# All transfers issued on one queue, and the last wait placed behind the closing barriers

The kernel runs on one core of a Trainium2 chip. The metric is the device time of one execution in microseconds, median of several runs; before the change 72.71 us.

Some words first. SP, ACT (ScalarE), VectorE, TensorE and GpSimd are the five engines; each works through its own list of instructions. SP, and here ACT too, issue transfers; 16 DMA engines then move the bytes in packets (those of the data are of 24,576 to 40,960 B in the kernel before). A transfer has landed when its semaphore, a counter that engines wait on, has been raised for all of it. At a barrier every engine waits for the others.

## The reference

A max-unpooling: every input element goes to one of the four places of a 2 x 2 block of the output, which `indices` names; the other three are zero.

```python
batch, channels, h, w = 16, 64, 32, 32            # kernel_size = 2
# x: float32 of that shape, indices: integers 0..3 (64 bit when they reach the kernel)
output = np.zeros((batch, channels, 2 * h, 2 * w), dtype=np.float32)
for b, c, i, j in ...:                            # cut: four nested loops
    idx = indices[b, c, i, j]
    output[b, c, 2 * i + idx // 2, 2 * j + idx % 2] = x[b, c, i, j]
```

In bytes: x 4.19 MB, indices 8.39 MB (the kernel reads all 64 bits and uses the low half), output 16.78 MB; 29.36 MB in all.

## The kernel before

The 1024 images lie on 128 partitions, eight per partition. SP loads x and then the last five images of indices; ACT loads the first three images of indices beside it. VectorE makes the output in 20 instructions, each the product of x and "index equals p" for one of the four places p. The output has four groups of two images; each is stored by SP with one transfer as soon as it is made. At the end SP waits for the stores, then two barriers over all engines close the program; those are added around the kernel and do not stand in its text.

```python
    with Program(nc) as program:
        program.first(nc.sync.dma_start(out=x_t, in_=x_v).then_inc(x_in, 16))
        program.first(nc.sync.dma_start(out=idx_t[:, cut:], in_=idx_v[:, cut:]).then_inc(idx_in[1], 16))
        program.first(nc.scalar.dma_start(out=idx_t[:, :cut], in_=idx_v[:, :cut]).then_inc(idx_in[0], 16))

        nc.vector.wait_ge(x_in, 16).then_inc(x_in, -16)
        for t in range(T):
            ...                    # cut: wait for idx_in at t = 0 and 3, for stored_0 at the last group
            for pidx in range(4):
                op = nc.vector.scalar_tensor_tensor(
                    out=o_c[:, k : k + n, :, pidx // 2, :, pidx % 2],
                    in0=idx_c[:, t : t + n], scalar=pidx, in1=x_c[:, t : t + n],
                    op0=mybir.AluOpType.is_equal, op1=mybir.AluOpType.mult)
            if k + n == G:
                op.then_inc(made, 1)

        for g in range(NG):
            nc.sync.wait_ge(made, g + 1)
            nc.sync.dma_start(out=out_v[g], in_=out_t[g]).then_inc(stored if g else stored_0, 16)
        nc.sync.sem_inc(made, -NG)
        nc.sync.wait_ge(stored, 16 * (NG - 1)).then_inc(stored, -16 * (NG - 1))
```

`program.first` puts a transfer ahead of the opening barrier, so that it starts at once: in the trace the issue of x starts at 0.00 us, the barrier's last semaphores at 1.2.

## Time and profile before

| | before |
|---|---|
| time, median (lowest to highest of 3) | 72.71 us (72.57 to 72.78) |
| the profiled execution: time / span | 72.79 / 71.00 us |
| part of the time outside the span | 1.79 us |
| VectorE busy | 35.6 us, half of the span |
| one packet of 32,768 B on one DMA engine | 1.213 us, 27.0 GB/s; 432 GB/s on 16 |

The span runs from the first recorded instruction to the end of the last one. The profile's lines on which the reading rests are in the prediction below; each "L" number is a line of the kernel that was profiled, so the same instruction has another number in another kernel.

### The profile page before, as it was taken

How to read it: one execution, taken by the hardware profiler on the slowest of the kernel's cores; microseconds unless marked ns; L12 is line 12 of the kernel's file. 1: busy time of each engine (PE TensorE's matmuls, PEld its weight loads, DVE VectorE, ACT ScalarE, POOL GpSimd, SP SyncE). 2: the span in 40 equal slices, each digit the busy share in tenths (PEclk: the TensorE clock that was granted, in tenths of full speed). 3: DMA queues.
4: the chain of work that ended last, by engine and by line, in shares of the span. 5: the costliest groups of instructions: out<-in, count | busy, mean ns of one | idle time of the engine just before them, and what ended most of it. 6: DMA issues, size and time to landing. Idle time of an engine off the chain costs nothing.

```text
span 71.0 us, 72 instructions
## 1 busy us (share of the span) xinstructions
DVE 35.6 (50%) x20; POOL 0.2 (0%) x4
## 2 busy tenths in 40 slices
DVE  0000000000089999999999999999999200000000
POOL 1000000000000000000000000000000000000000
DMA  9598997998988999879696989899898979696980
GB/s 277 240 434 378 517 498 314 443 462 378 563 369 369 462 577 438 369 314 572 295 591 295 517 369 517 369 425 462 369 517 351 535 314 572 295 591 295 517 369 0
DMA packets 1009, 29.36 MB, mean 414 GB/s; under 512 B 113, under 2 KB 113, under 8 KB 113
## 3 DMA queue, kind: packets, MB, share of 16 engines
q1 hardware_dynamic: 864, 26.21, 86.4%
q10 hardware_dynamic: 144, 3.15, 10.3%
q14 instruction: 1, 0.00, 0.0%
HBM read 12.58 MB, written 16.78 MB: 414 GB/s over the span
## 4 chain that ended last, share of the span: by engine, by line
DVE 45%; DVEq 4%; issue 1%
DVE out_t L127 45%; DVEq L175 4%
## 5 line engine op out<-in xcount | busy, mean ns | idle before, releaser
L127 DVE SCALAR_TENSOR_TENSOR out_t<-idx_t,x_t 128x2048 f32<-128x2048 int32 (+1 forms) x20 | 35.6, 1860 | 19.9 <-DVEq L116 19.9
L161 POOL MEMSET const-bfloat16-1.0<- 128x1 bf16 x1 | 0.1, 103 | 0.0
L161 POOL MEMSET const-uint8-127<- 128x1 uint8 x1 | 0.1, 102 | 0.0
L161 POOL MEMSET const-float32-1.0<- 128x1 f32 x1 | 0.1, 100 | 0.0
L161 POOL MEMSET const-float32-0.0<- 128x1 f32 x1 | 0.1, 99 | 0.2 <-issue 0.2
## 6 DMA issues: line engine op xcount, KB each, us to landing
out_dram<-out_t SPq DMA_DIRECT2D x4, 4096.0 KB, 13.5
idx_t<-in_indices_dram SPq DMA_DIRECT2D x1, 5120.0 KB, 31.2
x_t<-in_x_dram SPq DMA_DIRECT2D x1, 4096.0 KB, 19.5
idx_t<-in_indices_dram ACTq DMA_DIRECT2D x1, 3072.0 KB, 19.6
```

The lines of the kernel that those rows point to most:

```text
L127: op = nc.vector.scalar_tensor_tensor(out=o_c[:, k : k + n, :, pidx // 2, :, pidx % 2], in0=idx_c[:, t : t + n], scalar=pidx, in1=x_c[:, t ...
L161: nc = _bacc.Bacc("TRN2", target_bir_lowering=False, num_devices=1)
L175: with _tile.TileContext(nc) as tc:
```

## The change

Its intent is to let one engine issue all transfers in the order in which they are needed (x, three images of indices, five images, stores), and to let SP go through the closing barriers while the last stores still run, with the wait for them as SP's last instruction. The diff, with context cut:

```diff
+    def last(self, made):
+        def move(nc):
+            ins = self.block.instructions
+            at = next(k for k, i in enumerate(ins) if i.name == made.ins.name)
+            nc.main_func.blocks[-1].instructions.append(ins.pop(at))
+
+        self.nc.at_finalize(move)
...
         program.first(nc.sync.dma_start(out=x_t, in_=x_v).then_inc(x_in, 16))
-        program.first(
-            nc.sync.dma_start(out=idx_t[:, cut:], in_=idx_v[:, cut:]).then_inc(
-                idx_in[1], 16
+        for half, part in enumerate((slice(0, cut), slice(cut, None))):
+            program.first(
+                nc.sync.dma_start(out=idx_t[:, part], in_=idx_v[:, part]).then_inc(
+                    idx_in[half], 16
+                )
             )
-        )
-        program.first(
-            nc.scalar.dma_start(out=idx_t[:, :cut], in_=idx_v[:, :cut]).then_inc(
-                idx_in[0], 16
-            )
-        )
...
-        nc.sync.wait_ge(stored, 16 * (NG - 1)).then_inc(stored, -16 * (NG - 1))
+        program.last(
+            nc.sync.wait_ge(stored, 16 * (NG - 1)).then_inc(stored, -16 * (NG - 1))
+        )
```

## The prediction

> **What bounds the kernel now.** I read the page first (share of each engine, slices, queues), then the table of windows, the chain of waits, SP's own waits, and last the line and tile views of the closing instructions. The page:
>
> ```profile
> span 71.0 us, 72 instructions
> DVE 35.6 (50%) x20; POOL 0.2 (0%) x4
> ...
> DMA  9598997998988999879696989899898979696980
> ...
> HBM read 12.58 MB, written 16.78 MB: 414 GB/s over the span
> ```
>
> VectorE, the only computing engine, works half of the span; the DMA row is full from the third slice to the last but one. So this is a transfer kernel. The table of windows shows how even the transfers are (columns: stretch, length, VectorE and GpSimd busy, TensorE clock, DMA share, GB/s):
>
> ```profile
> 0.00:1.00 1.00, 0.00 (x0) 0.20 (x4) 1.00 0.00 0
> 1.00:2.90 1.90, 0.00 (x0) 0.00 (x0) 1.00 1.01 289
> 2.90:19.50 16.60, 0.00 (x0) 0.00 (x0) 1.00 1.04 449
> 19.50:31.20 11.70, 11.33 (x7) 0.00 (x0) 1.00 1.00 431
> 31.20:55.50 24.30, 24.27 (x14) 0.00 (x0) 1.00 1.01 434
> 55.50:69.50 14.00, 0.00 (x0) 0.00 (x0) 1.00 0.95 412
> 69.50:70.30 0.80, 0.00 (x0) 0.00 (x0) 1.00 0.01 0
> 70.30:71.00 0.70, 0.00 (x0) 0.00 (x0) 1.00 0.00 0
> ```
>
> A packet is booked whole in one stretch, so a stretch may be a few per cent off; the packet records say it better: every packet of 32,768 B takes 1.213 us and every one of 24,576 B takes 0.912 us, with no gap between packets of an engine, that is 27.0 GB/s on each of 16 engines, or 432 GB/s. All 29.36 MB at that rate need 67.95 us. The rest of the 71.0 us is the edges: 1.0 us until the first packet, a first packet that takes up to 2.33 us in place of 1.21, an offset of half a us between the engines, and the end. The reader is to see that only the two edges can be shortened; the 68 us between them hold the same bytes whatever their order.
>
> The page's chain of waits is of little use here:
>
> ```profile
> 41.63 2.83 DVEq L175
> 44.46 11.01 DVE out_t L127 x5
> ```
>
> It stops at VectorE's last result, at 55.5 us, and doesn't see the transfer behind it. SP's own waits and the two views of the end show the real one:
>
> ```profile
> SPq L144 <- SPq L144: 14.5, 1, 14.5
> SPq L175 <- PEq L175: 0.4, 2, 0.3
> ...
> L140 SPq DMA_DIRECT2D out_dram<-out_t x4: 333/338/347, 28.8 to 55.5; - x4
> ...
> DMA to landing us min/median/max: 12.6/13.5/14.8
> ...
> L144 SPq EVENT_SEMAPHORE  x1: 17/17/17, 70.3 to 70.3; - x1
> ...
> L175 POOLq EVENT_SEMAPHORE  x4: 17/17/17, 70.5 to 70.9; - x4
> ```
>
> The last store is issued at 55.5 us, lands 14.8 us later, at 70.3 us, and SP's wait for it passes at 70.3. Then come two closing barriers at 70.4 to 71.0 in which nothing moves. In the trace's records SP's wait ends at 70.343 and the last instruction of all, a barrier semaphore on TensorE's sequencer, at 71.002: 0.66 us.
>
> [...] from 2.9 to 19.1 us every DMA engine alternates a packet of x with one of the first indices, and the rate is the same 27 GB/s per engine that it has afterwards with SP's queue alone. [...] the last completion packet stands at 69.96 us and SP passes at 70.33, so 0.37 us of receipt stay with any order. [...] the profiled run took 72.79 us against a span of 71.0, so 1.79 us of the metric lie outside of it, and no run so far tells what they are.
>
> **The change part by part.**
>
> (a) The loads. Before, SP issues x (4.19 MB) and five images of indices (5.24 MB), ACT beside it three images of indices (3.15 MB). After, SP issues x, three images, five images. ACT loses one issue of 0.365 us; SP gets one more of about 0.4 us, ending near 1.3 us in place of 0.86. SP then arrives at the opening barrier at about 1.45 us, not 0.91. VectorE needs that barrier only at 19.6 us, so this costs nothing. VectorE's first instruction waits for both x and the first indices. Per engine these are 8 packets of 32 KiB and 8 of 24 KiB: 8 x (1.213 + 0.912) = 17.0 us of packets, interleaved or one behind the other. They end at about 19.1 to 19.4 us in both kernels; x now lands alone near 12.5 us in place of 19.5, but nobody uses it then. Worth to VectorE: 0, give or take 0.2.
>
> The five images end at 31.2 us in both. The first store is issued at 28.8 us, still ahead of the end of the loads; the four stores take 9.7 us each (8 packets per engine x 1.213 us), and are issued every 8.8 us, at 28.8, 37.9, 46.7 and 55.5. The last is issued 14.8 us ahead of its landing for 9.7 us of work: it waits some 4 us behind the third. So VectorE could even start 3 us later without an effect on the end. Order and queue are off the path. Sum of (a) in the steady part: 0.
>
> At the starting edge something might move. [...] the first packets of x take 1.67 to 2.33 us and not 1.21. If that is descriptors made in turn for two queues, the change gives back a part of about 0.5 us; if it is a first read that is slow anyway, nothing. I book -0.1 us.
>
> (b) SP's last wait. Before: wait at 70.33, then an SP drain, barrier one, barrier two, end at 71.00. After: SP passes both barriers right after the last issue, at about 56 to 57 us, beside the last store, which still has 13 us to run; then waits, and that is its last instruction. Removed from the path: 71.00 - 70.34 = 0.66 us on TensorE's queue, or 0.61 us if SP's own end counts (its last semaphore ended at 70.956). Added: 0; the wait itself (17 ns) was already there. The number of instructions and branches is the same.
>
> Sum: 72.71 - 0.66 - 0.1 = 71.95 us; the span from 71.00 to about 70.25. Against 72.71 that is -1.0%.
>
> **The rivals.**
>
> Rival 1: the tail is not in the metric as I read it. If the clock stops where the runtime has gathered all engines, then what four engines do after their last instruction could also move beside the last store, and the gain would exceed 0.66 us. For it: 1.79 us lie outside the span. Against it: SP is still last[...]. At most some 0.5 us more: 71.4. The opposite, that the barrier was already hidden, has nothing for it, because 0.66 us stand bare in the span; it would give 72.6.
>
> Rival 2: the start moves by more than I book. A clean first packet of 1.21 us on all engines, with descriptors not shared, could gain 0.5 us to 0.6 us: 71.45. For it: the first packets start at 1.00 to 2.00 us but end all at 2.90 to 3.40, as if held by one thing. Against it: that thing may be the first HBM access, which the change leaves.
>
> Rival 3: one queue is worse than two, for instance a gap where one transfer ends and the next begins[...]. Against it: in the trace the step from x to the five images on SP's queue shows 9 ns for the completion packet and no gap, and three stores stand in that queue behind each other at full rate. [...] With a gap of 0.3 us: 72.25.
>
> Rival 4: VectorE becomes the bound because its input lands later. It would need to start about 3 us later than 19.9; the byte count doesn't give that. 1 in 50; 73 or more.
>
> **Range and chances.** Rivals 1 and 2 pull down by up to 0.5 us each, rival 3 up by 0.3, and the median of three runs is good to 0.1 us (72.57 to 72.78). Hence 71.95 with 71.45 to 72.35 at 8 in 10. Faster by over 2% means under 71.26, a gain of 1.45 us: it needs 0.8 us beyond the tail, both rivals 1 and 2 together: 0.06. Slower by over 2% needs a stall the trace gives no hint of: 0.01. Within 2%: 0.93.
>
> **What would show it right or wrong.** Right: a span near 70.3; SP's last wait passing at 70.2 to 70.4 and being the last instruction; the barrier semaphores near 56 us; x landing at about 12.5 us and the first indices at about 19.5; VectorE starting at 19.6 to 20.0 and its 35.6 us unbroken; the same four landing times; packets of 1.213 us. Step (b) is wrong if the span falls by 0.66 us and the time doesn't, or the time falls by much more than the span. The starting edge is wrong if the first packets end clearly ahead of 2.9 us. The argument as a whole is wrong if the packets' rate differs with one queue or gaps appear between transfers.

## The result

| | before | after |
|---|---|---|
| time, median (lowest to highest of 4) | 72.69 us (72.57 to 72.78) | 71.60 us (71.46 to 71.86) |
| ratio, 95% interval | | 0.9855 (0.9824 to 0.9887) |
| the profiled execution: time / span | 72.79 / 71.00 us | 71.56 / 70.24 us |
| part outside the span | 1.79 us | 1.32 us |
| SP's last wait ends at | 70.343 us | 70.238 us |
| GpSimd's last instruction ends at | 70.914 us | 56.210 us |
| TensorE's last instruction ends at | 71.002 us | 56.298 us |

A ratio here is the mean time of one kernel's fast runs over that of the other's of the same rounds, so not quite the ratio of the medians quoted. The change gains 1.5%, about 1.1 us. The class is "within 2%".

The page of the changed kernel: VectorE's work is the same 35.6 us, the bytes are the same, and the span is shorter by 0.76 us.

```profile
span 70.2 us, 72 instructions
DVE 35.6 (51%) x20; POOL 0.2 (0%) x4
...
HBM read 12.58 MB, written 16.78 MB: 418 GB/s over the span
```

The windows of the changed kernel, in the stretches of the prediction (columns as there; the last but one is the DMA share, the last GB/s). From 1.0 to 69.5 us the rates differ by no more than a few packets that fall on one or the other side of a border; the 0.7 us without transfers at the end are gone.

```profile
1.00:2.90 1.90, 0.00 (x0) 0.00 (x0) 1.00 0.91 276
2.90:19.50 16.60, 0.00 (x0) 0.00 (x0) 1.00 1.04 450
19.50:31.20 11.70, 11.64 (x7) 0.00 (x0) 1.00 1.01 437
31.20:55.50 24.30, 23.96 (x14) 0.00 (x0) 1.00 1.00 432
55.50:69.50 14.00, 0.00 (x0) 0.00 (x0) 1.00 0.95 412
69.50:70.20 0.70, 0.00 (x0) 0.00 (x0) 1.00 0.01 0
```

The page's list of transfers (KB each, us from issue to landing), x and the three images of the kernel before first, then the changed kernel's loads. Before, x took 19.5 us and the three images 19.6 us, since their packets alternated (1.213 us for one of x, 0.912 for one of the images). Now x lands at 12.1 us, and nobody needs it then: VectorE also needs the three images, which land at 0.4 + 19.0 = 19.4 us. It starts at 19.56 us, before at 19.87.

```profile
x_t<-in_x_dram SPq DMA_DIRECT2D x1, 4096.0 KB, 19.5
idx_t<-in_indices_dram ACTq DMA_DIRECT2D x1, 3072.0 KB, 19.6
```

```profile
idx_t<-in_indices_dram SPq DMA_DIRECT2D x1, 5120.0 KB, 30.6
x_t<-in_x_dram SPq DMA_DIRECT2D x1, 4096.0 KB, 12.1
idx_t<-in_indices_dram SPq DMA_DIRECT2D x1, 3072.0 KB, 19.0
```

SP's own waits in the changed kernel (us in total, times, longest; L151 is the moved wait, L183 the closing barriers):

```profile
SPq L151 <- SPq L151: 14.0, 1, 14.0
SPq L183 <- PEq L183: 0.4, 2, 0.3
```

The line views of the moved wait and of the barriers in the changed kernel (count, duration in ns, first and last start in us). The wait still takes 14.0 us, but the barriers' GpSimd semaphores now stand at 55.8 to 56.2 us and not at 70.5 to 70.9, and L151 is the last thing of all.

```profile
L151 SPq EVENT_SEMAPHORE  x1: 17/17/17, 70.2 to 70.2; - x1
```

```profile
L183 POOLq EVENT_SEMAPHORE  x4: 17/17/17, 55.8 to 56.2; - x4
```

So the two traces show where the shorter span comes from. They do not show why the time fell by 1.1 us when the barriers' part in the span is only 0.66: the part outside the span fell too, from 1.79 to 1.32 us. That is the question of the experiments.

### The profile page after: what moved, and what is told of

Same layout as the page of the kernel before. It is cut to its first block, busy times and chain, and to the rows that moved or that the text cites. A ratio compares the mean times of both kernels' runs of the same rounds, so it can differ in the third digit from the quotient of the medians.

```text
span 70.2 us, 72 instructions
## 1 busy us (share of the span) xinstructions
DVE 35.6 (51%) x20; POOL 0.2 (0%) x4
## 4 chain that ended last, share of the span: by engine, by line
DVE 46%; DVEq 4%; issue 1%
DVE out_t L133 46%; DVEq L183 4%
## 5 line engine op out<-in xcount | busy, mean ns | idle before, releaser
L133 DVE SCALAR_TENSOR_TENSOR out_t<-idx_t,x_t 128x2048 f32<-128x2048 int32 (+1 forms) x20 | 35.6, 1857 | 19.6 <-DVEq L122 19.6
## 6 DMA issues: line engine op xcount, KB each, us to landing
x_t<-in_x_dram SPq DMA_DIRECT2D x1, 4096.0 KB, 12.1
```

The source lines that it names most:

```text
L133: op = nc.vector.scalar_tensor_tensor(out=o_c[:, k : k + n, :, pidx // 2, :, pidx % 2], in0=idx_c[:, t : t + n], scalar=pidx, in1=x_c[:, t ...
```

## The experiments

Twelve runs, in four calls on up to three chips (8, 6, 8 and 3); each ratio is against the kernel before in the same call. All outputs are right. "Outside" is the time less the span, as a mean over the runs with a span; the spans of the single runs are known to 0.1 us.

### Which part of the change gains

**The changed kernel again**, no edit, as the yardstick.

> The changed kernel once more, as the yardstick on this chip for the other runs of the call. All theories: some 1.05 us under the kernel before (ratio 0.9855 on record), a span near 70.2 to 70.5, and 1.3 to 1.4 us of the time outside the span (1.79 in the profiled run of the kernel before).

Measured: 71.60 us against 72.73, ratio 0.9841 (0.9825 to 0.9857), outside 1.32 us against a mean of 1.79 over the eleven runs of the kernel before (1.75 to 1.83). The gain and the smaller outside part are both steady.

**Only the wait moved**, loads as before:

```diff
-        nc.sync.wait_ge(stored, 16 * (NG - 1)).then_inc(stored, -16 * (NG - 1))
+        program.last(
+            nc.sync.wait_ge(stored, 16 * (NG - 1)).then_inc(stored, -16 * (NG - 1))
+        )
```

> Only the last wait moved behind the closing barriers; loads as before (ACT issues three images). Theory T (the tail makes all of it): ratio 0.985 to 0.987, span down by 0.66 us, time outside the span down from 1.79 to about 1.34. Theory A (ACT's missing transfer makes what lies outside the span shorter): only the span's 0.66 us, ratio 0.991, outside still 1.79. If the start gains 0.1 us by the loads, this run is 0.1 us slower than the changed kernel.

Measured: 71.69 us, ratio 0.9851 (0.9834 to 0.9868), outside 1.32 us. The moved wait alone makes 1.08 us of the changed kernel's 1.15 (means), and all of the smaller outside part. By the medians this run is 0.09 us slower than the changed kernel, which is what the expectation said of a start that gains 0.1 us; but the two intervals overlap, so the runs don't tell 0.1 us from nothing.

**Only the loads changed**, the wait ahead of the barriers as before:

```diff
-        program.last(
-            nc.sync.wait_ge(stored, 16 * (NG - 1)).then_inc(stored, -16 * (NG - 1))
-        )
+        nc.sync.wait_ge(stored, 16 * (NG - 1)).then_inc(stored, -16 * (NG - 1))
```

(against the changed kernel)

> Only the order of the loads and their issuer; SP waits for the stores ahead of the closing barriers as before. Theory T: ratio 0.998 to 1.001, outside the span 1.79 us. Theory A: ratio 0.993, outside the span about 1.34. Theory of the start (no second queue at the start, first packets quicker): 0.1 us or more off the span, ratio 0.998 or less.

Measured: 72.71 us, ratio 0.9996 (0.9982 to 1.001), outside 1.81 us. One queue in place of two, another order of landing, and ACT without a transfer are worth nothing that these runs can see: the interval is a gain of 0.13 us to a loss of 0.07, so a tenth of a microsecond is not excluded. The closing lines of this kernel look like those of the kernel before, with SP's wait (L150) at 70.2 and the barriers (L181) behind it, each from the view of its line:

```profile
L150 SPq EVENT_SEMAPHORE  x1: 17/17/17, 70.2 to 70.2; - x1
```

```profile
L181 POOLq EVENT_SEMAPHORE  x4: 17/17/17, 70.3 to 70.7; - x4
```

### Why the part outside the span shrinks

**All engines held to the end.** Added to the changed kernel (cut: the line that makes the semaphore `done`):

```diff
+        program.last(nc.sync.sem_inc(done, 4))
+        for engine in (nc.tensor, nc.vector, nc.scalar, nc.gpsimd):
+            program.last(engine.wait_ge(done, 1).then_inc(done, -1))
```

> The changed kernel, with the other four engines held to the end: after its wait SP adds 4 to a semaphore, and each of the four waits for it as its last instruction, about 0.05 to 0.1 us after SP. Theory E (0.45 us outside the span fell because four engines were done and out of the way 14 us earlier): outside the span back to about 1.79, time 72.1 to 72.2, ratio 0.993. Theory P (the part outside depends only on when SP is done): time only 0.05 to 0.1 us above the changed kernel, ratio 0.986 to 0.987, outside the span 1.3.

Measured: 72.28 us, ratio 0.9938 (0.992 to 0.9956), outside 1.82 us. Here no barrier follows SP's wait; its signal reaches the others within 0.14 us, and yet 0.7 us of the gain are gone. The lines of its end show that the four waits end together, right behind SP (L156 is the added wait; the profiled execution was the slowest of the six, hence 70.7 and not 70.4):

```profile
L156 POOLq EVENT_SEMAPHORE  x1: 17/17/17, 70.7 to 70.7; - x1
...
L156 PEldq EVENT_SEMAPHORE  x1: 51/51/51, 70.7 to 70.7; - x1
```

So it matters to the time outside the span when the other engines have their last instruction. The next four runs ask which of them. In each, one other engine makes the last wait alone, and SP is done at 56 us like the rest:

```diff
         program.last(
-            nc.sync.wait_ge(stored, 16 * (NG - 1)).then_inc(stored, -16 * (NG - 1))
+            nc.tensor.wait_ge(stored, 16 * (NG - 1)).then_inc(stored, -16 * (NG - 1))
         )
```

(and likewise with `nc.scalar`, `nc.vector`, `nc.gpsimd`)

> The changed kernel, but TensorE's queue and not SP makes the last wait, alone at the end; SP is done at about 56 us. Theory S (one engine's way from its last instruction to the end of the measured time is longer than the others'): if it is TensorE's, outside the span 1.75 to 1.85 us and time 72.1; if not, 1.3 or less and 71.6. Theory N (0.48 us come from several engines ending at once, no matter which): 1.3 us, time 71.6, here and with every other engine.

> As before, with ScalarE's queue as the one that waits last. Theory S: outside the span 1.75 to 1.85 us if ScalarE's way is the long one, else 1.3 or less. Theory N: 1.3 us, time 71.6.

> As before, with VectorE's queue as the one that waits last. Theory S: outside the span 1.75 to 1.85 us if VectorE's way is the long one, else 1.3 or less. Theory N: 1.3 us, time 71.6.

> As before, with GpSimd's queue as the one that waits last. Theory S: outside the span 1.75 to 1.85 us if GpSimd's way is the long one, else 1.3 or less. Theory N: 1.3 us, time 71.6. An engine with a way under 1.3 us would make a kernel faster than the changed one by the difference.

Measured; "way out" is the profiled execution's time less the end of that engine's last instruction in its trace, which is known to some 0.01 us (SP's is 1.32 to 1.34 in the six runs with SP last). What the measured time holds ahead of the first recorded instruction, if anything, is in it too, the same for every engine; so only the differences between the ways belong to the engines:

| the engine that waits last | median us | ratio (95%) | its last instruction ends at | time of that execution | way out |
|---|---|---|---|---|---|
| SP (the changed kernel) | 71.60 | 0.9855 (0.9824 to 0.9887) | 70.238 | 71.56 | 1.32 |
| VectorE | 71.78 | 0.9866 (0.9853 to 0.988) | 70.350 | 71.80 | 1.45 |
| ScalarE | 71.94 | 0.9886 (0.987 to 0.9903) | 70.442 | 71.94 | 1.50 |
| TensorE | 72.17 | 0.9917 (0.9903 to 0.993) | 70.525 | 72.19 | 1.67 |
| GpSimd | 72.23 | 0.9927 (0.9914 to 0.9941) | 70.325 | 72.20 | 1.88 |

Neither theory was right as written. Theory N (it doesn't matter which engine) falls: the same 17 ns wait costs over half a us more on GpSimd than on SP. Theory S expected one engine with the long way and 1.3 us for all others; there are five different ways. GpSimd's is the longest and SP's the shortest, so the change chose the best engine for its last wait. The line view of the run with GpSimd, with its head, shows that its span is about as short as the changed kernel's, and still it takes 72.2 us:

```profile
core 0 of [0], span 70.3 us
...
L151 POOLq EVENT_SEMAPHORE  x1: 17/17/17, 70.3 to 70.3; - x1
```

**All but GpSimd held to the end**, to test whether the ways stand side by side (the latest counts) or add to each other:

```diff
-        program.last(nc.sync.sem_inc(done, 4))
-        for engine in (nc.tensor, nc.vector, nc.scalar, nc.gpsimd):
+        program.last(nc.sync.sem_inc(done, 3))
+        for engine in (nc.tensor, nc.vector, nc.scalar):
             program.last(engine.wait_ge(done, 1).then_inc(done, -1))
```

(against the run with all held)

> As the run in which all were held to the end, but GpSimd is not held and is done at about 56 us. Theory M (each engine has its own fixed way out, SP 1.32, VectorE 1.48, ScalarE 1.52, TensorE 1.64, GpSimd 1.87 us after its own last instruction, and the latest of the five sums is the time): TensorE decides, with its last instruction some 0.14 us after SP's, so 70.44 + 1.64 = 72.08 us, ratio 0.990 to 0.991, outside the span 1.64. Theory N (several engines ending at once slow each other): 72.2 or more, outside the span 1.8 as when all five were held.

Measured: 72.11 us, ratio 0.9913 (0.9898 to 0.9927; expected 0.990 to 0.991, so just above it), outside 1.68 us. With GpSimd let go, the time falls by 0.17 us against the run with all held, and the outside part is TensorE's, not GpSimd's. The view of the added wait, with its head:

```profile
core 0 of [0], span 70.4 us
...
L156 PEldq EVENT_SEMAPHORE  x1: 51/51/51, 70.4 to 70.4; - x1
```

So the latest of the sums counts, as theory M had it before the run. The ways of the table above reproduce the executions that did not go into it (the first four rows are the test; the last two only repeat SP's way):

| profiled execution | the sum that is latest | us | measured |
|---|---|---|---|
| before | GpSimd 70.914 + 1.875 | 72.79 | 72.79 |
| only the loads | GpSimd 70.752 + 1.875 | 72.63 | 72.62 |
| all held | GpSimd 70.697 + 1.875 | 72.57 | 72.58 |
| all but GpSimd held | TensorE 70.419 + 1.665 | 72.08 | 72.08 |
| only the wait | SP 70.253 + 1.322 | 71.58 | 71.58 |
| changed, again | SP 70.302 + 1.322 | 71.62 | 71.63 |

(1.875, 1.665 and 1.322 are the ways of GpSimd, TensorE and SP with one more digit.) In the kernel before, TensorE ended the span at 71.002, but 71.002 + 1.665 = 72.67 is less than GpSimd's 72.79: the instruction that ended the span was not the one that ended the time. What happens in these 1.3 to 1.9 us no trace here shows; that the ways differ, and by how much, is shown, the reason is open.

### Can the start be shortened

With the middle full (packets of 1.213 us without a gap) and the end settled, only the first 3 us are left: the first packet starts at 1.0 us and the first packet of an engine takes up to 2.3 us where later ones take 1.2. What the expectations below name as the cause, descriptors or slow first reads, is the author's guess; no trace here shows either at work.

**x in two parts, 16 partitions first, then 112**, and **x in two halves of 64 partitions, on SP and ACT at once** (both against the changed kernel; VectorE then waits for 32 and not 16):

```diff
-        program.first(nc.sync.dma_start(out=x_t, in_=x_v).then_inc(x_in, 16))
+        for rows in (slice(0, 16), slice(16, P)):
+            program.first(
+                nc.sync.dma_start(out=x_t[rows], in_=x_v[rows]).then_inc(x_in, 16)
+            )
```

```diff
+        for engine, rows in ((nc.sync, slice(0, 64)), (nc.scalar, slice(64, P))):
+            program.first(
+                engine.dma_start(out=x_t[rows], in_=x_v[rows]).then_inc(x_in, 16)
+            )
```

> The changed kernel with the load of x in two transfers on SP: 16 partitions first, then 112. Is the slow start (first packets from 1.0 to 2.0 us on, all done only at 2.9 to 3.4) the making of many descriptors for the first transfer? Theory D (it is): the first packets, one per engine, start at about 0.7 us and close together, and the whole stream moves ahead by 0.3 us or more, ratio under 0.981. Theory H (the first reads are slow whatever asks for them): same first packets, ratio 0.984 to 0.986 like the changed kernel. Theory G (the second issue costs more than the first saves): a gap after the first packets, ratio 0.988 or more.

> The changed kernel with x's load split by partitions, 64 on SP and 64 on ACT, issued at the same time. Theory D: [...] first packets start by 1.5 us at the latest on all engines, 0.1 to 0.3 us gained, ratio 0.980 to 0.983. Theory H: ratio 0.984 to 0.986, first packets done at 2.9 to 3.4 us again. ACT's last instruction stays at about 56 us, so the end is as in the changed kernel.

Measured: 81.16 us, ratio 1.1148 (1.113 to 1.1167), and 81.58 us, ratio 1.1208 (1.1188 to 1.1228). They are 9.6 and 10.0 us slower than the changed kernel, which none of the theories had, and they say nothing about the start. The windows of the run with two halves show what happened (columns as above; the changed kernel's line for the same stretch stands last): until x has landed, at about 22.9 us, the transfers run at half of the rate, and afterwards at the usual one.

```profile
5.00:19.00 14.00, 0.00 (x0) 0.00 (x0) 1.00 1.02 225
19.00:23.00 4.00, 0.00 (x0) 0.00 (x0) 1.00 0.64 221
23.00:40.00 17.00, 10.50 (x6) 0.00 (x0) 1.00 1.02 441
```

```profile
5.00:19.00 14.00, 0.00 (x0) 0.00 (x0) 1.00 1.05 453
```

The DMA share is full at 225 GB/s: the engines are not idle, each packet is slow. In the packet records a 32,768 B packet of x takes 2.35 us (median) and not 1.21, and eight of them per engine lose 8 x 1.14 = 9.1 us, most of the 10.0; the first packet also starts 0.33 us later (1.36 against 1.03 us). Nor were the two halves, though they stand in two queues, at work side by side in the two stretches looked at: at 7.0 to 7.5 us all 16 engines work on packets of ACT's queue, at 9.5 to 10.0 us all on SP's. Why a packet to one half of the partitions takes twice as long, no trace here shows. In the run with 16 and 112 partitions a packet takes between 1.7 and 4.3 us until x has landed, and the rate from 5 to 19 us is 241 GB/s; whether the cause is the same there is not shown.

**x in two parts of all 128 partitions, one image first, then seven:**

```diff
-        program.first(nc.sync.dma_start(out=x_t, in_=x_v).then_inc(x_in, 16))
+        for cols in (slice(0, N), slice(N, None)):
+            program.first(
+                nc.sync.dma_start(out=x_t[:, cols], in_=x_v[:, cols]).then_inc(
+                    x_in, 16
+                )
+            )
```

> The question of the slow start again, without the fault of the two runs before it (a transfer to a part of the 128 partitions ran at half the rate): the changed kernel with x in two transfers on SP, both to all 128 partitions, first one image (packets of 4 KiB), then seven (28 KiB). Theory H (the first packet of an engine is slow whatever its size): first packets take about 1 us, all the rest as in the changed kernel, ratio 0.984 to 0.987. Theory D (large first packets are held up while descriptors are still given out): first packets done near 1.2 to 2.2 us, the stream 0.3 us or more ahead, ratio 0.981 or less. Theory G (the second transfer's descriptors come later and leave a gap): ratio 0.989 or more.

Measured: 71.79 us, ratio 0.9885 (0.9862 to 0.9909). That the stream moves ahead by 0.3 us (theory D) is excluded. The interval takes in what theory H and theory G expect, and two of the six executions had spans of 70.8 us where the others had 70.3 to 70.5; so the time doesn't tell those two apart. In its trace the 16 packets that start first end at 1.27 to 2.19 us, as theory D expected, after 0.16 to 1.05 us each, and not after about 1 us as theory H did; but nothing behind them moves ahead, and the three images land as late as before (VectorE's second wait passes at 19.48 us; 19.45 in the changed kernel). What holds up the start stays open; no version tried brings the stream forward, and none is faster than the changed kernel.

## Why the prediction was right or wrong

The time, 71.6 us, lies inside the range (71.45 to 72.35) and the class was right, but the middle of the range was 0.35 us too high. That it lay inside is partly the width of the range: a tail of 0.46 us was missing from the sum, and the 0.1 us booked for the start, which no run shows, may have hidden part of that. Most of the signs it named came out (span 70.24 us, SP's wait last at 70.24, barrier semaphores near 56, x landing at 12.1, packets of 1.213 us, and from the last completion packet, 69.87 us, to SP's wait passing, 70.22, about the same time as before: 0.35 us, 0.37 before); VectorE's start, 19.56 us, fell just short of its 19.6 to 20.0. But so did its sign against step (b), "the time falls by much more than the span": 0.47 us more. By the steps:

- **The steady part of (a), 0: right.** The run with only the loads changed gives 0.9996. Packets of 1.213 us and no gaps, in one queue as in two; rivals 3 and 4 (a gap between transfers, VectorE as the bound) did not come.
- **The start in (a), -0.1 us: not shown.** The trace after has VectorE's start 0.3 us earlier and SP's last wait 0.1 us earlier, which looks like the predicted step. But over the traces VectorE starts at 19.48 to 19.90 us with one queue (nine traces with x in one transfer) and at 19.70 and 19.87 with two, so the pair says little. The interval of the loads alone is -0.13 to +0.07 us, which holds both 0 and -0.1. The reason offered for it, two queues at once (the issues overlapped before, SP's at 0.00 to 0.38 us, ACT's at 0.12 to 0.49), fell: with one queue the first packets still end at 2.94 to 3.31 us (2.90 to 3.40 before). That descriptors were made in turn was a guess that no trace shows. One reading was off, too: of the sixteen first packets of x before, the one that starts last, at 2.00 us, took the usual 1.21 us; "1.67 to 2.33" holds for the other fifteen.
- **(b), the moved wait, -0.66 us: right in the mechanism, mis-sized.** Measured -1.08 us alone (means of 71.69 against 72.77 us). The failed step is "0.66 us on TensorE's queue, or 0.61 us if SP's own end counts": it took the end of the span, or SP's, for the end of the time. Before, GpSimd's last instruction counted, 0.57 us behind SP's wait (70.914 less 70.343) and with a way out of 1.88 us; after, SP's own wait counts with a way of 1.32 us. 0.57 + 0.55 = 1.12 us.
- **Rival 1 was the half that was missing**, and it was booked at nothing in the sum. It named the right place, "what four engines do after their last instruction", and the right size, "at most some 0.5 us more" (0.46 beyond the 0.66), though it is GpSimd's way against SP's that makes it, not something that all four engines do. The argument against it, "SP is still last", was the mistake: being last on SP alone is cheaper (1.32 us outside the span) than being last on all five (1.82 with all held).
- With the tail put right, 71.95 - 0.46 = 71.49 us with the booked start, 71.59 without it; measured 71.60 (71.46 to 71.86), which doesn't tell the two apart.

## What to carry to other kernels

Where the metric counts more than the recorded span, compare time less span in two kernels before trusting a sum of span parts; here 0.47 us of 1.1 were there (1.79 less 1.32). A last wait that only has to keep the program from ending belongs behind whatever all engines must still do together, and on the engine whose way out is shortest (here SP with 1.32 us, while GpSimd with 1.88 would have given back more than half of the gain). When the transfers run without a gap at a constant packet time (here 1.213 us), changing their order or their issuer has little to gain (here nothing that the runs could see), but splitting one by partitions halved its rate here (225 GB/s against 453).
